# Two changes to a hybrid decoder block: counting in two steps, and the down products at a distance of four FFN tiles

## The chip, the cores and the metric

One core of a Trainium2 chip runs the whole kernel in one launch. The metric is the device time of that launch in microseconds (us). The engines are TensorE (PE; its weight loads are shown as PEld), VectorE (DVE), ScalarE (ACT), GpSimd (POOL) and SyncE (SP), which issues every DMA here. Runs of one kernel lie close together, so the median of three is compared.

## What is computed

One decoder layer for 2048 tokens of width 1024, in float32:

```python
h = rms(x, norm1_g); proj = h @ w_in                      # u, q, k, v, qi, ki, wi, gates
y_ssm = s5_branch(u, ...)                                 # state-space scan, then a GLU
iscore = sum_h relu(qi_h . ki) * wi_h                     # indexer scores, causal
idx = top_k(iscore, 256)                                  # per query, 256 keys
y_att = softmax(q . k[idx]) @ v[idx]                      # 8 heads on the chosen keys
x = x + (sigmoid(g_ssm) * (y_ssm @ w_proj_ssm)
         + sigmoid(g_att) * (y_att @ w_proj_attn)) @ w_out
h2 = rms(x, norm2_g)
x = x + (silu(h2 @ w_ffn_gate) * (h2 @ w_ffn_up)) @ w_ffn_down   # d_ff = 2816
```

## The kernel before

**Products.** Each float32 operand is kept as a rounded part and a remainder, and each product is three TensorE passes (`mm3`, line 406): high by high, high by low, low by high.

**Stages.** `phase1` computes the projections. Then three generators are interleaved by a planner (`Pace`, line 52): the state-space branch, the attention branch, and the dense part. The planner keeps an estimated time for each engine; each generator yields a condition, and the planner lets the first one go on whose condition holds by these estimates. The result is a fixed order of instructions for each engine; the engines follow it and wait on semaphores. A generator that yields `idle("DVE")` goes on when the estimated DVE time is at most `AHEAD` (2.5, later 7 us) ahead of PE's.

**The top-k search.** For a group of four query tiles, `topk` computes the scores `S` of a tile of 128 queries (tile i has (i+1)*128 keys), and finds the 256th largest score of each query by a search over 31 bits. Each bit needs a count of the scores at or above a trial value. Two tiles of a group are "wide": ACT counts them by a Sign activation with an accumulator, and DVE updates the trial value (`un`, then `tr`). The other two are "narrow": DVE counts them, on the high 16 bits of the scores (`H`, as bf16) and then on the low 16 (`H`, as uint16). `count` (line 849) is one `tensor_scalar` over the whole width, with an accumulator; its elementwise output goes to a scratch tile `jkd`. There are four searches: tiles 2 and 3, 4 to 7, 8 to 11, 12 to 15, with narrow widths of 384, of 640 and 768, of 1152 and 1280, and of 1664 and 1792 keys. After a search, `fin` steps (a count of the scores above the threshold, a scan to rank ties, some elementwise steps) make a bias row, and attention of that group follows.

**The dense part.** `block` handles 512 tokens (`tb` 0 to 3): products of the two branches with their projections (`f<-act,ww`), w_out (`f<-ww,mg`), the second norm (its tiles are `ha`, `hb`, `hh`), then 22 FFN tiles f of 128 columns. `up(f, acts)` makes the 48 products of gate and up for one f, and ACT and DVE turn them into an activation tile `at` (DVE step `t`, ACT cast, DVE remainder). `down(acts, last)` multiplies a pair of activation tiles with the two matching rows of w_ffn_down (48 products) and DVE adds each result to `x1`. The loop over c issues up(2c), then down of the pair before, then up(2c+1). Three `at` tiles are kept (pool `fa`).

**Weights.** `weights` lists the loads of a block in one queue, in the order of use; `Rings` hands them out to two rings of buffers: `w` with three tiles, `d` (w_ffn_down, a pair of rows each) with one tile (two in block 3). The queue is first in, first out: a load whose ring is full holds back those behind it. In block 0 a weight is loaded raw, split by POOL, ACT or DVE into its two parts and stored; the later blocks load the stored copies `wc`.

Of the kernel before, what the change touches and what calls it, by code (L numbers as in the profile page):

```python
# [18 lines left out]
ALU = mybir.AluOpType  # L19
# [15 lines left out]
NF = DFF // 128  # L35
# [330 lines left out]
class Block:  # L366
# [431 lines left out]
    def topk(self, st, groups, KL):  # L798

        nc, at, idle = self.nc, self.pace.at, self.pace.idle  # L800
# [35 lines left out]
        S = {}  # L836
        states = []
        for j, (tiles, wide) in enumerate(groups):
# [3 lines left out]
            n = len(tiles)  # L842
# [3 lines left out]
        self.spare_banks = 4  # L846
        jka, jkd = (qp.tile([128, L], BF16, name=n, tag="R") for n in ("jka", "jkd"))

        def count(x, i, t, c):

            nc.vector.tensor_scalar(jkd[:, :(i + 1) * 128], x, t, 0.0, op0=ALU.is_ge, op1=ALU.add, accum_out=c)

        def search(j, tiles, b, wide):

# [83 lines left out]
        for j, (tiles, b) in enumerate(states):  # L938
            n = len(tiles)
            tr = qp.tile([128, n], I32, name="trf")  # L940
            gt = qp.tile([128, n], F32, name="gt")
            fx = qp.tile([128, n], I32, name="fx")
            sg = qp.tile([128, n], I32, name="sg")
            sg2 = qp.tile([128, n], F32, name="sg2")
            ss = qp.tile([128, n], F32, name="ssum")
            nT = qp.tile([128, n], F32, name="nT")
            bf = b.bitcast(F32)
            yield idle("DVE")
            for q, i in enumerate(tiles):
                W = (i + 1) * 128  # L950
                nc.vector.tensor_scalar(jkd[:, :W], S[i], bf[:, q:q + 1], 0.0, op0=ALU.is_gt, op1=ALU.add,
                                        accum_out=gt[:, q:q + 1])
            nc.vector.tensor_scalar(fx, gt, float(TOPK), None, op0=ALU.is_ge)
            nc.vector.tensor_scalar(sg2, b, 0.0, None, op0=ALU.is_ge)
            nc.vector.tensor_scalar(sg, sg2, 2.0, -1.0, op0=ALU.mult, op1=ALU.add)
            nc.vector.tensor_tensor(tr, b, sg, op=ALU.add)
            nc.vector.copy_predicated(b, fx, tr)
            nc.vector.tensor_scalar(nT, bf, -1.0, None, op0=ALU.mult)

            todo = deque(enumerate(tiles))  # L960
            halves = deque()

            def sign():
                nonlocal order
                if todo:
                    q, i = todo.popleft()
                    W = (i + 1) * 128
                    sv, ev = (fin[:, order % 2, z, :W] for z in range(2))
                    order += 1
                    nc.scalar.activation(sv, S[i], AF.Sign, bias=nT[:, q:q + 1], scale=1.0,  # L970
                                         accum_out=ss[:, q:q + 1])
                    halves.append((q, i, W, sv, ev))
            yield idle("ACT", nT)
            sign()
            while halves:
                q, i, W, sv, ev = halves.popleft()
                yield idle("DVE", ss)
                sign()
                nc.vector.tensor_scalar(ev, sv, 0.0, None, op0=ALU.is_equal)
                nc.vector.tensor_tensor_scan(S[i], ones.to_broadcast([128, W]), ev, 0.0, op0=ALU.mult, op1=ALU.add)  # L980
                yield idle("DVE")
                r = qp.tile([128, 1], F32, name="r")
                r2 = qp.tile([128, 1], F32, name="r2")
                nc.vector.tensor_scalar(r2, gt[:, q:q + 1], -1.0, float(TOPK), op0=ALU.mult, op1=ALU.add)
                nc.vector.scalar_tensor_tensor(r, ss[:, q:q + 1], float(W - TOPK), gt[:, q:q + 1],
                                               op0=ALU.add, op1=ALU.subtract)
                nc.vector.tensor_scalar(r, r, -1.0, None, op0=ALU.mult)
                nc.vector.copy_predicated(r2, fx[:, q:q + 1], r)
                nc.vector.scalar_tensor_tensor(ev, S[i], r2, ev, op0=ALU.is_gt, op1=ALU.mult)
                yield idle("DVE")  # L990
                nc.vector.tensor_tensor(ev, ev, sv, op=ALU.subtract)
                nc.vector.tensor_scalar(ev, ev, 0.0, -BIG, op0=ALU.max, op1=ALU.mult)
                yield at("SP", ev)
                nc.sync.dma_start(self.bias_d[i], ev)
# [646 lines left out]
    def weights(self):  # L1641

        a = self.a
        items = []
        for ct in range(KD):
            items.append(("w", lambda raw, ct=ct: [
                (raw[:, i * 512:(i + 1) * 512].rearrange("p (k c) -> p k c", k=4),
                 a[w][0, :, ct * 128:(ct + 1) * 128].rearrange("(k p) c -> p k c", p=128))
                for i, w in enumerate(("w_proj_ssm", "w_proj_attn"))]))
        for cg in range(4):  # L1650
            for b in range(2):
                items.append(("w", lambda raw, cg=cg, b=b: [
                    (raw.rearrange("p (k c) -> p k c", k=4),
                     a["w_out"][0, b * 512:(b + 1) * 512, cg * 256:(cg + 1) * 256]
                     .rearrange("(k p) c -> p k c", p=128))]))
        for f in range(NF):
            for w in ("w_ffn_gate", "w_ffn_up"):
                items.append(("w", lambda raw, f=f, w=w: [
                    (raw.rearrange("p (k c) -> p k c", k=KD),
                     a[w][0, :, f * 128:(f + 1) * 128].rearrange("(k p) c -> p k c", p=128))]))  # L1660

            n = f if f % 2 == 0 else f + 1 if f == NF - 1 else 0
            for q in range(max(n - 2, 0), n):
                items.append(("d", lambda raw, q=q: [(raw, a["w_ffn_down"][0, q * 128:(q + 1) * 128])]))
        copies = [self.dram.tile([128, 2, 1024], F32, name=f"wc{i}") for i in range(len(items))]
        return [(kind, parts, copy, tb > 0) for tb in range(NB) for (kind, parts), copy in zip(items, copies)]
# [8 lines left out]
    def block(self, tb, bigp, ld, nps, nd):  # L1675

        nc, a, at = self.nc, self.a, self.pace.at
        n = TB
# [5 lines left out]
        with ExitStack() as st:  # L1684
# [28 lines left out]
            with ExitStack() as sm:  # L1713
# [123 lines left out]
                yield ready(*hT)  # L1837
                yield from up0(0, (2, 3))
                self.pace.tight = False
            ap = self.pool(st, "fa", 3)  # L1840
            tp = self.pool(st, "ft", 2)
            ld.ring("d", self.pool(st, "fd", nd), nd, 2)

# [63 lines left out]
                if last:  # L1907
                    out(nt - 1)

            prev = None  # L1910
            for c in range(NF // 2):
                acts = []
                for f in (2 * c, 2 * c + 1):
                    acts.append(ap.tile([128, 2, n], F32R, name="at"))
                    yield from up(f, acts[-1])
                    if f % 2 == 0 and prev:
                        yield from down(prev, False)
                prev = acts
            if tb + 1 < NB:
                self.act = [self.load_branch(bigp, br, tb + 1) for br in range(1 + (self.attended >= 4 * (tb + 2)))]  # L1920
            yield from down(prev, True)
            more.close()
            self.lent = False
            del ld.pools["d"]
# [78 lines left out]
```

## Time and profile before

| | |
|---|---|
| median of 3 runs | 3424.11 us (3422.59 to 3427.55) |
| profiled execution | 3425.84 us, of which the span is 3424.1 us |
| busy, share of the span | PE 93%, PEld 78%, DVE 63%, ACT 37%, POOL 19% |
| mean granted TensorE clock | 0.971 of full speed |

```profile
PE   6999989898978999987899999989899999999999
DVE  5565686665886666889777667987766664322222
POOL 3323676521222212343100000001000000000000
PEclk8999999999999999998999999989999999999999
```

Each digit is the busy share of one fortieth of the span (85.6 us) in tenths; PEclk is the granted TensorE clock in tenths of full speed. PE has work nearly all the time, and it dips where DVE is fullest. The searches lie at about 390 to 470 us, 800 to 1000 us, 1405 to 1700 us and 2120 to 2390 us; blocks 0 to 3 start at 984, 1648, 2303 and 2957 us.

### The profile page before, as it was taken

The numbers are of one execution on the slowest core, as the hardware profiler recorded it, in microseconds if no ns is written. First come the engines' busy times: TensorE is split into PE (matmuls) and PEld (weight loads), VectorE is DVE, ScalarE is ACT, GpSimd is POOL, SyncE is SP. The second block draws the span as 40 slices with busy tenths as digits, with TensorE's granted clock in tenths as the row PEclk, the third lists the DMA queues.
The fourth block names the chain that finished last, engine by engine and source line by source line (L and its number), as shares of the span: only waits on it lengthen the run. The fifth ranks groups of instructions, "written<-read, shape, count | busy, mean of one in ns | idle before, by whom it ended". The sixth has DMA issues, their size and how long they took to land. (4 is left out here: it accounts for less than half of the span.)

```text
span 3424.1 us, 43974 instructions
## 1 busy us (share of the span) xinstructions
PE 3179.7 (93%) x16292; PEld 2684.6 (78%) x16292; DVE 2150.5 (63%) x4299; ACT 1262.8 (37%) x2192; POOL 638.6 (19%) x631
## 2 busy tenths in 40 slices
PE   6999989898978999987899999989899999999999
PEld 5889768677757887775788887768788888798887
DVE  5565686665886666889777667987766664322222
ACT  3141545454732444463024444761234342010000
POOL 3323676521222212343100000001000000000000
PEclk8999999999999999998999999989999999999999
DMA  4834433445368656566762334456453333755544
GB/s 134 250 114 117 127 106 108 157 121 156 108 222 289 225 179 226 198 239 249 262 225 112 140 108 171 165 209 227 183 187 131 115 110 141 302 207 200 205 165 183
DMA packets 321527, 605.68 MB, mean 177 GB/s; under 512 B 52896, under 2 KB 205216, under 8 KB 290592
## 3 DMA queue, kind: packets, MB, share of 16 engines
q1 hardware_dynamic: 321312, 602.86, 50.3%
q8 instruction: 129, 2.11, 0.2%
q14 instruction: 86, 0.70, 0.1%
HBM read 434.71 MB, written 166.89 MB: 176 GB/s over the span
## 5 line engine op out<-in xcount | busy, mean ns | idle before, releaser
L206 PE MATMUL f<-h,ww 128*128 128x512 f32 (+1 forms) x4416 | 1011.6, 383 | 3.9 <-DVE x L206 2.2
L206 PEld LDWEIGHTS f<-h,ww 128*128 128x128 f32 x4416 | 800.1, 190 | 160.1 <-POOL ww L206 3.4
L206 PE MATMUL f<-wd,at 128*128 128x512 f32 x2112 | 529.5, 402 | 63.9 <-ACT at L206 34.9
L206 PEld LDWEIGHTS f<-wd,at 128*128 128x128 f32 x2112 | 402.3, 194 | 160.0 <-ACT at L206 27.9
L206 PE MATMUL gps<-hT,gw 128*128 128x512 f32 x1536 | 383.6, 400 | 11.2 <-ACT gsg L206 10.0
L206 ACT ACTIVATE jka<-S,tr 128x1024 bf16<-128x1024 f32 (+6 forms) x217 | 305.8, 1409 | 181.5 <-DVE tr L206 135.8
L206 PEld LDWEIGHTS gps<-hT,gw 128*128 128x128 f32 x1536 | 285.3, 191 | 75.2 <-ACT gsg L206 12.1
L206 DVE TENSOR_TENSOR x<-f,x 128x512 f32<-128x512 f32 x352 | 237.3, 687 | 90.9 <-PE f L206 90.2
L206 DVE SCALAR_TENSOR_TENSOR t<-t,f 128x512 f32<-128x512 f32 (+1 forms) x124 | 82.4, 664 | 329.8 <-PE f L206 285.0
L206 PE MATMUL mm<-w,hT 128*128 128x512 f32 (+1 forms) x1152 | 282.0, 402 | 7.5 <-DVE hT L206 7.3
L206 PEld LDWEIGHTS mm<-w,hT 128*128 128x128 f32 x1152 | 242.1, 241 | 32.9 <-DVE hT L206 9.0
L206 DVE TENSOR_TENSOR tl<-pt,th 128x512 fp32r<-128x512 f32 (+1 forms) x288 | 184.2, 659 | 133.3 <-ACT th L206 132.0
L206 ACT CAST th<-pt 128x512 fp32r<-128x512 f32 (+1 forms) x288 | 155.9, 563 | 233.7 <-PE pt L206 231.7
L206 PE MATMUL f<-act,ww 128*128 128x512 f32 x768 | 189.8, 409 | 29.1 <-DMA act<-act 8.8
L206 POOL TENSOR_TENSOR g<-g,g 128x512 f32<-128x512 f32 x31 | 40.0, 1291 | 916.8 <-issue 553.1
L206 PE MATMUL f<-ww,mg 128*128 128x256 f32 x1536 | 193.5, 288 | 17.5 <-DMA ww<-wc 6.7
L206 PEld LDWEIGHTS f<-ww,mg 128*128 128x128 f32 x1536 | 190.3, 196 | 19.8 <-issue 7.7
L206 PEld LDWEIGHTS f<-act,ww 128*128 128x128 f32 x768 | 150.9, 199 | 67.9 <-issue 10.9
L206 ACT ACTIVATE P<-P,m 128x1024 f32<-128x1024 f32 (+7 forms) x192 | 172.2, 900 | 69.2 <-DVE m L206 68.8
L206 PE MATMUL lg<-kk,q 128*128 128x512 f32 (+1 forms) x640 | 183.9, 389 | 3.4 <-DMA kk<-kk 2.8
L206 ACT ACTIVATE t<-f 128x512 f32<-128x512 f32 (+1 forms) x92 | 53.0, 576 | 332.0 <-PE f L206 331.9
L206 ACT CAST at<-t 128x512 fp32r<-128x512 f32 (+1 forms) x92 | 55.3, 601 | 324.9 <-DVE t L206 324.9
(355 smaller groups left out, 4512.4 us busy)
## 6 DMA issues: line engine op xcount, KB each, us to landing
ww<-wc SPq DMA_DIRECT2D x180, 1024.0 KB, 5.0
wd<-wc SPq DMA_DIRECT2D x66, 1024.0 KB, 8.3
wc<-ww SPq DMA_DIRECT2D x60, 1024.0 KB, 7.8
raw<-in_w_in_dram SPq DMA_DIRECT2D x104, 256.0 KB, 3.4
wc<-wd SPq DMA_DIRECT2D x22, 1024.0 KB, 7.4
x<-in_x_dram SPq DMA_DIRECT2D x32, 512.0 KB, 5.5
gate<-gsg SPq DMA_DIRECT2D x64, 256.0 KB, 2.2
g<-gate SPq DMA_DIRECT2D x64, 256.0 KB, 5.2
```

The costliest lines, as they stand in the source:

```text
L206: return f(*args, **kw)
```

## The change

`count` works in two steps. A `tensor_scalar` without an accumulator compares the first half of the keys and writes 0 or 1 into `jkd`; a `scalar_tensor_tensor` compares the second half, adds that `jkd` elementwise, and accumulates the sum. The count after a search (is greater) goes the same way.

In the dense part two pairs of activation tiles wait in a queue: after up(2c) the product of the pair before the last one is issued, and after the last up both remaining pairs follow, one behind the other. Five `at` tiles are kept. The loads of w_ffn_down stand two f later in the queue, and the last four rows stand together at its end.

```diff
--- before.py
+++ after.py
@@ -846,9 +846,11 @@
         self.spare_banks = 4
         jka, jkd = (qp.tile([128, L], BF16, name=n, tag="R") for n in ("jka", "jkd"))
 
-        def count(x, i, t, c):
-
-            nc.vector.tensor_scalar(jkd[:, :(i + 1) * 128], x, t, 0.0, op0=ALU.is_ge, op1=ALU.add, accum_out=c)
+        def count(x, i, t, c, op=ALU.is_ge):
+
+            h = (i + 1) * 64
+            nc.vector.tensor_scalar(jkd[:, :h], x[:, :h], t, None, op0=op)
+            nc.vector.scalar_tensor_tensor(jkd[:, h:2 * h], x[:, h:], t, jkd[:, :h], op0=op, op1=ALU.add, accum_out=c)
 
         def search(j, tiles, b, wide):
 
@@ -947,9 +949,7 @@
             bf = b.bitcast(F32)
             yield idle("DVE")
             for q, i in enumerate(tiles):
-                W = (i + 1) * 128
-                nc.vector.tensor_scalar(jkd[:, :W], S[i], bf[:, q:q + 1], 0.0, op0=ALU.is_gt, op1=ALU.add,
-                                        accum_out=gt[:, q:q + 1])
+                count(S[i], i, bf[:, q:q + 1], gt[:, q:q + 1], ALU.is_gt)
             nc.vector.tensor_scalar(fx, gt, float(TOPK), None, op0=ALU.is_ge)
             nc.vector.tensor_scalar(sg2, b, 0.0, None, op0=ALU.is_ge)
             nc.vector.tensor_scalar(sg, sg2, 2.0, -1.0, op0=ALU.mult, op1=ALU.add)
@@ -1659,8 +1659,7 @@
                     (raw.rearrange("p (k c) -> p k c", k=KD),
                      a[w][0, :, f * 128:(f + 1) * 128].rearrange("(k p) c -> p k c", p=128))]))
 
-            n = f if f % 2 == 0 else f + 1 if f == NF - 1 else 0
-            for q in range(max(n - 2, 0), n):
+            for q in range(max(f // 2 * 2 - (4 if f % 2 == 0 else 2), 0), f - 2 if f % 2 == 0 else NF if f == NF - 1 else 0):
                 items.append(("d", lambda raw, q=q: [(raw, a["w_ffn_down"][0, q * 128:(q + 1) * 128])]))
         copies = [self.dram.tile([128, 2, 1024], F32, name=f"wc{i}") for i in range(len(items))]
         return [(kind, parts, copy, tb > 0) for tb in range(NB) for (kind, parts), copy in zip(items, copies)]
@@ -1837,7 +1836,7 @@
                 yield ready(*hT)
                 yield from up0(0, (2, 3))
                 self.pace.tight = False
-            ap = self.pool(st, "fa", 3)
+            ap = self.pool(st, "fa", 5)
             tp = self.pool(st, "ft", 2)
             ld.ring("d", self.pool(st, "fd", nd), nd, 2)
 
@@ -1907,18 +1906,19 @@
                 if last:
                     out(nt - 1)
 
-            prev = None
+            pairs = deque()
             for c in range(NF // 2):
                 acts = []
                 for f in (2 * c, 2 * c + 1):
                     acts.append(ap.tile([128, 2, n], F32R, name="at"))
                     yield from up(f, acts[-1])
-                    if f % 2 == 0 and prev:
-                        yield from down(prev, False)
-                prev = acts
+                    if f % 2 == 0 and len(pairs) == 2:
+                        yield from down(pairs.popleft(), False)
+                pairs.append(acts)
             if tb + 1 < NB:
                 self.act = [self.load_branch(bigp, br, tb + 1) for br in range(1 + (self.attended >= 4 * (tb + 2)))]
-            yield from down(prev, True)
+            yield from down(pairs.popleft(), False)
+            yield from down(pairs.popleft(), True)
             more.close()
             self.lent = False
             del ld.pools["d"]
```

The planner makes another order of it. Three places follow; every engine issues the same arithmetic on PE as before.

On PE, in block 0, the first scores of the second attention (`lg<-kk,q`; `f<-ww,mg` are the w_out products, `f<-h` those of gate and up). Before:

```order
L206 MATMUL f<-act_9345,ww 128x512 x12
L206 MATMUL f<-act_9313,ww 128x512 x12
L206 MATMUL f<-act_9345,ww 128x512 x12
L206 MATMUL f<-ww,mg 128x256 x168
L206 MATMUL lg<-kk,q 128x512 x2
L206 MATMUL lg<-kk,q 128x256 x2
L206 MATMUL f<-ww,mg 128x256 x12
L206 MATMUL lg<-kk,q 128x512 x2
```

Now the same place reads:

```order
L206 MATMUL f<-h_9803,ww 128x512 x12
L206 MATMUL f<-h_9802,ww 128x512 x12
L206 MATMUL f<-h_9803,ww 128x512 x12
L206 MATMUL f<-h_9802,ww 128x512 x12
L206 MATMUL lg<-kk,q 128x512 x2
L206 MATMUL lg<-kk,q 128x256 x2
L206 MATMUL f<-h_9803,ww 128x512 x6
L206 MATMUL lg<-kk,q 128x512 x2
```

They stood among the w_out products of block 0 and stand now among its first gate and up products; all that depends on them (the second attention, and the third search behind it) moved back by about as much.

On DVE, in block 2, the second norm (`ha`, `hb`, `hh` are normed rows, `h` their transposed remainders, `x` an update of the residual; `fin` and `S<-ones,fin` belong to the steps behind the fourth search, `jkd` to a count). Before:

```order
L206 SCALAR_TENSOR_TENSOR hb<-x_20251,rr_21027,gB 128x1024
L206 SCALAR_TENSOR_TENSOR x_20251<-f,x_20251 128x2x256
L206 TENSOR_TENSOR h_20591<-f,h_20591 128x4x128
L206 TENSOR_TENSOR h_20592<-f,h_20592 128x4x128
L206 TENSOR_TENSOR h_20591<-f,h_20591 128x4x128
L206 TENSOR_TENSOR h_20592<-f,h_20592 128x4x128
L206 TENSOR_SCALAR ss_21116<-ss_21116 128x1
L206 TENSOR_SCALAR ss_21121<-ss_21121 128x1
L206 SCALAR_TENSOR_TENSOR hh<-x_20251,rr_21117,gB 128x1024
L206 SCALAR_TENSOR_TENSOR hh<-x_20251,rr_21122,gB 128x1024
L206 TENSOR_SCALAR fin<-fin 128x1920
L206 SCALAR_TENSOR_TENSOR S_18668<-ones,fin 128x1920
```

Now the same place reads:

```order
L206 SCALAR_TENSOR_TENSOR hb<-x_20334,rr_21166,gB 128x1024
L206 SCALAR_TENSOR_TENSOR x_20334<-f,x_20334 128x2x256
L206 TENSOR_TENSOR h_20688<-f,h_20688 128x4x128
L206 TENSOR_TENSOR h_20689<-f,h_20689 128x4x128
L206 TENSOR_TENSOR h_20688<-f,h_20688 128x4x128
L206 TENSOR_TENSOR h_20689<-f,h_20689 128x4x128
L206 TENSOR_SCALAR ss_21255<-ss_21255 128x1
L206 TENSOR_SCALAR ss_21260<-ss_21260 128x1
L206 SCALAR_TENSOR_TENSOR hh<-x_20334,rr_21256,gB 128x1024
L206 SCALAR_TENSOR_TENSOR hh<-x_20334,rr_21261,gB 128x1024
L206 TENSOR_SCALAR jkd<-H_19591,tf_19537 128x832
L206 SCALAR_TENSOR_TENSOR jkd,cnt_19536<-H_19591,tf_19537,jkd 128x832
```

The fourth search ended ahead of this norm, and a scan over 1920 keys stood in it; now the search still runs there and a count of two steps stands in its place.

On SP, at the end of block 2, the loads of w_ffn_down (`wd`), of the next block's weights (`ww`) and of the next block's branch activations (`act0`, `act1`); `out` stores the result, `g` loads gates. Before:

```order
L206 DMA wd_25472<-wc77_9305 128x2x1024
L206 DMA ww_25502<-wc78_9306 128x2048
L206 DMA ww_25533<-wc79_9307 128x2048
L206 DMA wd_25628<-wc80_9308 128x2x1024
L206 DMA wd_25628<-wc81_9309 128x2x1024
L206 DMA ww_25631<-wc0_9228 128x2048
L206 DMA ww_25660<-wc1_9229 128x2048
L206 DMA ww_25689<-wc2_9230 128x2048
L206 DMA act0_25694<-act3_185 128x2x512 x4
L206 DMA act1_25699<-att3_189 128x2x512 x4
L206 DMA out_0_dram<-x1_20251 128x1024 x4
L206 DMA g0_25791<-gate0_1_135 128x512
```

Now the same place reads:

```order
L206 DMA wd_25689<-wc79_9321 128x2x1024
L206 DMA act0_25837<-act3_185 128x2x512 x4
L206 DMA att3_189<-yh_25899 128x4x128
L206 DMA att3_189<-ya_24715 128x4x128
L206 DMA wd_25935<-wc80_9322 128x2x1024
L206 DMA wd_25935<-wc81_9323 128x2x1024
L206 DMA ww_25938<-wc0_9242 128x2048
L206 DMA ww_25940<-wc1_9243 128x2048
L206 DMA ww_25942<-wc2_9244 128x2048
L206 DMA out_0_dram<-x1_20334 128x1024 x4
L206 DMA g0_26032<-gate0_1_135 128x512
L206 DMA act1_26034<-att3_189 128x2x512 x4
```

The last pair of `wd` loads stood ahead of the last up and stands now behind `act0`, right before the next block's first weights; `act1` stood ahead of the stores and stands now behind them.

## Rows read from the trace of the kernel before

**Rows 1.** Page, busy time: busy us (share of the span), instructions.

```profile
PE 3179.7 (93%) x16292; PEld 2684.6 (78%) x16292; DVE 2150.5 (63%) x4299; ACT 1262.8 (37%) x2192; POOL 638.6 (19%) x631
```

**Rows 2.** Stretches: length, then busy PE, PEld, DVE, ACT, POOL, clock, DMA share, GB/s.

```profile
380.00:520.00 140.00, 125.68 (x615) 97.49 (x614) 114.36 (x311) 73.07 (x164) 97.46 (x157) 1.00 0.33 97
1406.00:1648.00 242.00, 197.96 (x798) 156.99 (x797) 217.14 (x388) 114.60 (x149) 96.35 (x46) 0.91 0.66 230
1648.00:1791.00 143.00, 131.84 (x801) 118.37 (x802) 96.45 (x166) 23.09 (x39) 13.49 (x12) 0.96 0.66 241
2120.00:2303.00 183.00, 160.30 (x676) 129.32 (x675) 170.64 (x350) 130.84 (x137) 0.30 (x1) 0.95 0.50 189
2303.00:2459.00 156.00, 136.72 (x801) 122.25 (x802) 115.34 (x173) 30.75 (x45) 13.50 (x12) 0.92 0.59 215
2957.00:3092.00 135.00, 129.60 (x803) 116.30 (x802) 35.84 (x55) 17.07 (x31) 13.43 (x12) 0.99 0.69 258
```

**Rows 3.** Timeline of PE in block 3: start, us, engine, operation, [idle before, releaser].

```profile
3091.74 11.04 PE L206 MATMUL f<-wd,at 128*128 128x512 f32 x48
...
3124.38 11.04 PE L206 MATMUL f<-wd,at 128*128 128x512 f32 x48
```

**Rows 4.** Timeline of PE in block 1, during the fourth search.

```profile
2120.30 21.95 PE L206 MATMUL f<-h,ww 128*128 128x512 f32 x96
...
2286.20 12.60 PE L206 MATMUL f<-wd,at 128*128 128x512 f32 x45 [9.06 <-ACT at L206]
```

**Rows 5.** Timeline of PE, last down products of block 0 and of block 2.

```profile
1633.75 13.20 PE L206 MATMUL f<-wd,at 128*128 128x512 f32 x45 [15.54 <-ACT at L206]
...
2946.30 10.74 PE L206 MATMUL f<-wd,at 128*128 128x512 f32 x45 [0.82 <-ACT at L206]
```

**Rows 6.** DVE by form, 2120 to 2303 us: count | busy us, mean ns.

```profile
L206 DVE TENSOR_SCALAR_CACHE_REDUCE jkd<-H,tr 128x1792 bf16<-128x1792 bf16 x15 | 31.1, 2076 | 0.2
...
L206 DVE SCALAR_TENSOR_TENSOR tr<-un,tr 128x1 int32<-128x1 int32 x59 | 9.4, 160 | 2.0
```

**Rows 7.** DVE by form, 1406 to 1648 us.

```profile
L206 DVE SCALAR_TENSOR_TENSOR tr<-un,tr 128x1 int32<-128x1 int32 x62 | 38.8, 626 | 2.1
L206 DVE TENSOR_SCALAR_CACHE_REDUCE jkd<-H,tr 128x1280 bf16<-128x1280 bf16 x15 | 23.1, 1539 | 0.1
```

**Rows 8.** Timeline of DVE, two `fin` steps over 2048 keys.

```profile
2390.15 0.69 DVE L206 TENSOR_SCALAR fin<-fin 128x2048 bf16<-128x2048 bf16 x1 [0.97 <-ACT fin L206]
...
2395.90 2.35 DVE L206 SCALAR_TENSOR_TENSOR fin<-S,r,fin 128x2048 bf16<-128x2048 f32 x1
```

**Rows 9.** DVE by form, 380 to 520 us: the same two steps, narrower.

```profile
L206 DVE SCALAR_TENSOR_TENSOR fin<-S,r,fin 128x384 bf16<-128x384 f32 x1 | 0.6, 618 | 0.0
...
L206 DVE TENSOR_SCALAR fin<-fin 128x512 bf16<-128x512 bf16 x2 | 0.7, 336 | 2.7 <-ACT fin L206 2.7
```

**Rows 10.** Timeline of DVE and POOL from 1449 us, in the third search.

```profile
1449.65 1.89 POOL L206 TENSOR_TENSOR ww<-raw,zeros 128x1024 fp32r<-128x1024 f32 x1 [8.49 <-PE f L206]
1449.77 1.54 DVE L206 TENSOR_SCALAR_CACHE_REDUCE jkd<-H,tr 128x1280 bf16<-128x1280 bf16 x1
...
1451.62 2.41 POOL L206 TENSOR_TENSOR ww<-raw,ww 128x1024 fp32r<-128x1024 f32 x1
...
1451.87 2.18 DVE L206 SCALAR_TENSOR_TENSOR tr<-un,tr 128x1 int32<-128x1 int32 x1
```

**Rows 11.** Timeline of SP at the end of block 2.

```profile
2933.95 1.18 SPq L206 DMA_DIRECT2D wd<-wc  x2
```

**Rows 12.** DMA issues from 2930 to 2990 us: KB each, median us to landing.

```profile
wd<-wc SPq DMA_DIRECT2D x2, 1024.0 KB, 6.2
...
act<-att SPq DMA_DIRECT2D x4, 512.0 KB, 10.4
```

**Rows 13.** Timeline of DVE and PE in the norm of block 2.

```profile
2420.25 4.16 DVE L206 TENSOR_TENSOR_SCAN S<-ones,fin 128x1920 f32<-128x1920 f32 x1
...
2425.05 1.97 PE L206 MATMUL f<-ident,hh 128*128 128x128 f32 x8 [5.91 <-DVE h L206]
```

## Prediction

> **What bounds the kernel now.** I read the page's busy times first: PE is busy 93% of the span [rows 1], so the change can only pay where PE waits or runs at a lower granted clock. Then a table of stretches [rows 2]: the two late searches stand out, 198 us of PE work in 242 us and 160 in 183, at a mean granted clock of 0.91 and 0.95 (mostly the level of 2.4 GHz, in part 1.2), with DVE busy for 217 and 171 of them. Undisturbed, PE needs 32.64 us for a pass of two ups and a down, 144 products (from 3091.74 to 3124.38) [rows 3], or 0.2267 us a product. By that the 798 products of the third search's stretch are worth 181 us, so 61 are lost there; the 676 of the fourth's are worth 153, so 30 are lost. Block starts without a search take 135 us, with one 143 and 156 [rows 2]: 8 and 21 lost.
>
> Next, which wait ends last. At the ends of blocks 0 and 1 PE waits 15.54 and 9.06 us for the activation tile of the last f [rows 4, 5], whose DVE step stands behind counts. In the passes ahead of it PE waits for banks that DVE has not emptied: from 2120.30 to 2286.20 less the 9.06 are 156.8 us, and the 627 products in it (four passes, 48 and 3) are worth 142.1; 14.7 are lost.
>
> **The counts.** A one-pass count takes 2.08 us at 1792 keys and 1.54 at 1280 [rows 6, 7], about 1.05 ns a key, so 1.94 at 1664, 1.40 at 1152, 0.60 at 384. No row shows the two new steps; the nearest are the `fin` steps. A tensor_scalar of bf16 took 0.34 us at 512 and 0.69 at 2048, a scalar_tensor_tensor 0.62 at 384 and 2.35 at 2048 [rows 8, 9]. On lines through these, half of 1792 keys costs 0.42 + 1.15 = 1.57, a saving of 0.50; 1664 saves 0.45, 1280 0.29, 1152 0.23, and 384 costs 0.26 + 0.42 = 0.68, 0.08 more. Half of the counts read uint16, and for a dense uint16 tensor_scalar there is no row. Its bounds are the bf16 line (0.42) and the scalar_tensor_tensor's (1.15), with which the count would be 0.2 slower; I take 0.42, since it reads as many bytes. The Trainium skill, "VectorE: DVE Perf Modes", "What auto-detection actually checks", goes by 16-bit type and step and not by bf16, which would give the same; no run here shows it. Over 31 bits and two tiles DVE gets back 29 us in the fourth search, 16 in the third, some 4 in the second, and loses 2.5 in the first.
>
> **What speaks against it.** POOL works for 97 of 140 us in the first search and 96 of 242 in the third, and for 0.3 of 183 in the fourth [rows 2]. A `tr` step, a scalar_tensor_tensor of one element a partition, takes 160 ns in the fourth search and 626 in the third [rows 6, 7]. One began 0.25 us into a POOL subtraction and ended with it, after 2.18 us. The one-pass count that began 0.12 us into another POOL step took its usual 1.54 [rows 10]. So two-input DVE steps are held while POOL works, and the one-pass count is not. The second new step has two inputs and is exposed; I take the first to be exposed too, since it is of the fast form. The Trainium skill states the rule ("SBUF — State Buffer", "SBUF: two separate sides"): a DVE operation that uses both ports, or reads two SBUF inputs, and a GpSimd operation exclude each other for their whole length; the traces agree with it for `tr` (626 against 160 ns). By the rule both steps are held, which is the slower rival below; were it not so, the hold terms here would be zero.
>
> The hold is 0.47 us for one exposed step at the third search's POOL share; a count has two, the second usually just behind the end of the hold, so 0.47 to 0.94 for the pair. I take 0.47, the row as it is. In the first search a count then loses 0.08 and some 0.5 by the same row: over 33 counts 20 us on DVE. Other PE work is interleaved there, DVE is busy 114 of 140 us, and I let 8 of the 20 reach PE (0 to 20).
>
> **What moves.** The second attention begins among the first gate and up products instead of the w_out products, some 65 us of PE work later, and the third search with it. By the order 50 of its 66 counts stood ahead of the end of block 0 and 16 in the start of block 1; now 30 and 36. Of the fourth search's counts 44 of 66 stood in block 1, now 29, and 37 fall into the start of block 2.
>
> - Third search in block 0: 61 us lost now, 45 without the 15.54. For 30 counts of 50 that is 27, plus hold 30 x 0.47 = 14 less the saving 30 x 0.26 = 8: 33. At the end the last two downs stand together. The first needs an older activation tile, and its 10.9 us cover the late DVE step. The second needs `wd`, whose one buffer is free only when the first has ended, and which is split anew there: POOL took 1.89 and 2.41 us for the two parts of such a tile [rows 10], the pair has two tiles, so 4.3 us shared out and 8.6 in a row; I take 6. 39 instead of 61: **-22** (-45 to +5).
> - Start of block 1: 8 lost with 16 counts, now 36 and the activation steps of the wide tiles: 14. **+6** (-5 to +20).
> - Fourth search in block 1: 30 lost now, 21 without the 9.06. For 29 counts of 44 it is 14; DVE, busy 171 of 183, gets 14 us free there, and I take half of the 14, 7. At the end `wd` is loaded: the two loads landed 6.2 us after their issue (median, rows 12) when they went out 12 us ahead of the product that waits [rows 5, 11]; now they go out when their buffer falls free, behind the first down, with the activation loads in flight, and PE waits 8 (6 to 10.4, the slowest median there). 15 instead of 30: **-15** (-25 to 0).
> - Start of block 2: 21 lost, of which 5.91 behind one scan of 4.16 us in the norm [rows 13]. The scans are gone from it, counts of 1.5 us stand there: **-6** (-20 to +10).
> - The `fin` steps of the third and fourth search now lie between ups and downs, with scans of 4 us ahead of evictions: **+4** (0 to 10).
> - End of block 2: 0.82 us of wait and a little more now [rows 5], then the `wd` loads as above: **+6** (4 to 10).
> - Start of block 3: `act1` was issued ahead of the last down; now it stands behind the stores on SP, since the last attention ends later. It landed 10.4 us after issue [rows 12]; the two products ahead of its first use cover 24 x 0.2267 = 5.4, SP's issues add 2: **+7** (0 to 10).
> - Start of block 0: 19 counts of the second search and its `fin` steps move into it. No row prices that: **+4** (-5 to +15).
> - Last block: both activation tiles are long ready at the end: **-1**.
>
> In all 8 - 22 + 6 - 15 - 6 + 4 + 6 + 7 + 4 - 1 = -9 us. Against the profiled execution's 3425.84 us that is 3416.8; it lay 1.7 above the median, so the forecast is **3415 us**. PE's arithmetic is the same, so everything else stays.
>
> **The rivals.**
> (a) POOL's hold decides (slower). Place: the first three searches. Each of the two steps is held, and POOL's weight splits are held in turn, so weights come late for PE. Price: the first search's whole 20 instead of 8, 7 in the second, 28 instead of 14 in the third, and 8 for late weights: 41 more, 3456. It decides once a two-step count in the third search takes over 1.9 us on average in block 0. For it: 626 against 160 ns. Against it: other PE work fills the first search.
> (b) The search's savings don't reach PE (near no change, or a little slower): the wide tiles on ACT set its length, the planner fills DVE as before, and the loss per pass stays. Then the fourth search gives 8 instead of 15, the third 14 instead of 22, block 2's start nothing: 3436 at worst, 3428 if one of the three holds. For it: ACT is busy 131 of 183 us. Were the uint16 step slow, the outcome is this one too: the change then does not make counts shorter.
> (c) The waits for activations were the root of more: with them gone DVE's backlog stops hurting, third search -35, fourth -22, block 2's start -12: 3389.
>
> **How the numbers follow.** About 0.2%, 7 us, is what a measurement of this kernel can tell from no change. The forecast has 0.50, its own range 3395 to 3428 (faster 0.36, same 0.12, slower 0.02). (a) has 0.20, slower. (b) has 0.20, of which 0.09 is same and 0.11 slower. (c) has 0.10, faster. Faster 0.46, same 0.21, slower 0.33. The range 3383 to 3449 takes in (b), nearly all of (c) and the lower half of (a).
>
> **What would show it.** In the profile after: `jkd` tensor_scalar of 0.4 and scalar_tensor_tensor of 1.1 us at 832 and 896 keys, and longer means where POOL works; no wait for `at` ahead of the last downs, but one for `wd` of 6 to 10 us at the ends of blocks 1 and 2 and a shorter one in block 0; a wait for `act1` at the start of block 3; passes in the fourth search of under 35 us. It is wrong if the passes stay at 36, if the first search's stretch grows by more than 15 us, or if block 0 ends later than 1650 us.

## The result, and the profile after

The changed kernel takes 3391.95 us (median of 4 runs, 3387.57 to 3394.26) against 3425.83 us of the kernel before in the same set: a ratio of 0.9898, 95% interval 0.988 to 0.9915. It is 34 us faster. 9 us faster was forecast: the time lies in the whole range (3383 to 3449), and some 3 us below the forecast's own part of it (3395 to 3428). Its page, busy times, for [rows 1]:

```profile
PE 3179.1 (94%) x16292; PEld 2687.4 (79%) x16292; DVE 2118.4 (62%) x4540; ACT 1277.2 (38%) x2210; POOL 622.4 (18%) x620
```

PE does the same work in 33 us less span. Where they went is read from the starts of the four blocks on PE, in both traces; each part holds the same number of products in both:

| part | before, us | after, us | difference | forecast |
|---|---|---|---|---|
| up to block 0 | 984.5 | 989.6 | +5.1 | +8 |
| block 0 | 663.3 | 642.4 | -20.9 | -18 |
| block 1 | 655.5 | 636.4 | -19.1 | -7 |
| block 2 | 653.6 | 656.0 | +2.4 | +2 |
| block 3 to the end | 467.2 | 466.4 | -0.8 | +6 |

(The forecast's +4 for the `fin` steps is shared between blocks 1 and 2.) The stretches that answer to [rows 2], after: length, busy PE, PEld, DVE, ACT, POOL, clock, DMA share, GB/s. They are the first search, the third from its first counts to the end of block 0, the start of block 1, and the fourth search from its first counts to the end of block 1.

```profile
380.00:520.00 140.00, 127.12 (x587) 98.64 (x586) 118.51 (x336) 70.16 (x155) 97.70 (x153) 0.94 0.32 94
...
1470.00:1632.00 162.00, 133.30 (x534) 105.18 (x532) 149.30 (x306) 90.12 (x116) 69.62 (x30) 0.92 0.68 240
1632.00:1798.00 166.00, 154.31 (x896) 137.19 (x897) 119.55 (x282) 46.24 (x69) 13.48 (x12) 0.96 0.60 223
2160.00:2268.00 108.00, 100.17 (x429) 81.61 (x428) 88.38 (x241) 82.74 (x87) 0.84 (x1) 0.97 0.60 225
```

At 0.2267 us a product, 162 - 534 x 0.2267 = 41 us are lost in the third search in block 0 (61 before, 39 forecast), and 108 - 429 x 0.2267 = 11 in the fourth in block 1 (30 before, 15 forecast). The new steps in that fourth search, DVE by form (count | busy us, mean ns):

```profile
L206 DVE SCALAR_TENSOR_TENSOR jkd<-H,tr,jkd 128x896 bf16<-128x896 bf16 x12 | 13.8, 1151 | 0.4
L206 DVE SCALAR_TENSOR_TENSOR tr<-un,tr 128x1 int32<-128x1 int32 x38 | 6.1, 160 | 1.3
...
L206 DVE TENSOR_SCALAR jkd<-H,tr 128x896 bf16<-128x896 bf16 x12 | 5.4, 449 | 0.1
```

The first step on uint16, DVE by form, 2268 to 2434 us:

```profile
L206 DVE TENSOR_SCALAR jkd<-H,tf 128x896 bf16<-128x896 uint16 x16 | 7.2, 452 | 0.5
```

A count of 1792 keys takes 0.45 + 1.15 = 1.60 us (forecast 1.57) for 2.08 [rows 6]. uint16 takes the short time too, as the Trainium skill has it in "VectorE: DVE Perf Modes", "What auto-detection actually checks": 452 ns beside 449.

The ends of the blocks, for [rows 4, 5], timeline of PE:

```profile
1609.18 0.51 PE L206 MATMUL f<-wd,at 128*128 128x512 f32 x1 [2.03 <-POOL wd L206]
1611.68 1.22 PE L206 MATMUL f<-wd,at 128*128 128x512 f32 x2 [2.00 <-POOL wd L206]
1614.05 0.80 PE L206 MATMUL f<-wd,at 128*128 128x512 f32 x1 [1.15 <-POOL wd L206]
1618.27 11.92 PE L206 MATMUL f<-wd,at 128*128 128x512 f32 x44 [3.43 <-DVE un L206]
...
2253.91 1.62 PE L206 MATMUL f<-wd,at 128*128 128x512 f32 x3 [5.47 <-DVE un L206]
2256.46 12.15 PE L206 MATMUL f<-wd,at 128*128 128x512 f32 x45 [0.94 <-DMA wd<-wc]
...
2908.60 1.62 PE L206 MATMUL f<-wd,at 128*128 128x512 f32 x3 [5.36 <-DMA wd<-wc]
2911.15 12.47 PE L206 MATMUL f<-wd,at 128*128 128x512 f32 x45 [0.93 <-DMA wd<-wc]
...
2933.87 0.97 PE L206 MATMUL f<-act,ww 128*128 128x512 f32 x3 [1.92 <-DMA act<-att]
```

Beside the wait at 1618.27, timeline of DVE:

```profile
1617.01 1.21 DVE L206 TENSOR_TENSOR wd<-raw,wd 128x1024 fp32r<-128x1024 f32 x1
```

No last product waits for its activation tile any more. It waits for `wd` instead. In blocks 1 and 2 that is 6.4 and 6.3 us, for the two loads in turn (`un`, named at 2253.91, is no input of these products; the loads, issued from 2248.5 on, landed 5.3 and 7.3 us later). In block 0 it is 8.6 us in four pieces: three behind POOL's parts of the split, and 3.43 for the second tile's remainder, which stands behind counts on DVE and ends at 1618.22 (`un` is again no input). At the start of block 3 the `act<-att` waits are 1.9 us and less.

So far all of the forecast's signs but one, the shorter `wd` wait in block 0, could be read as confirmed. The experiments show that the cause was another one.

### The profile page after: what moved, and what is told of

Its sections match the earlier page's. It is cut to its first block, busy times and chain, and to the rows that moved or that the text cites. A ratio compares the mean times of both kernels' runs of the same rounds, so it can differ in the third digit from the quotient of the medians.

```text
span 3390.8 us, 44218 instructions
## 1 busy us (share of the span) xinstructions
PE 3179.1 (94%) x16292; PEld 2687.4 (79%) x16292; DVE 2118.4 (62%) x4540; ACT 1277.2 (38%) x2210; POOL 622.4 (18%) x620
## 5 line engine op out<-in xcount | busy, mean ns | idle before, releaser
L206 PE MATMUL f<-wd,at 128*128 128x512 f32 x2112 | 521.1, 399 | 42.8 <-DVE un L206 16.0
L206 ACT ACTIVATE jka<-S,tr 128x1536 bf16<-128x1536 f32 (+5 forms) x217 | 305.6, 1408 | 193.6 <-DVE tr L206 119.2
```

The lines of the kernel that those rows point to most:

```text
L206: return f(*args, **kw)
```

## The experiments

**The theories.** *Counts*: shorter counts give DVE time back in the late searches. *Distance*: the activation waits were the root. *Order*: the gain is the new order of instructions, since the planner prices a count by its form, and the two forms have other prices. These lines of the planner (87 to 95) set the price; on DVE r is 1.05 ns a column, and `short` holds where the operands are of 16 bits:

```python
cost = size * r + c
...
if eng == "DVE" and op in ("tensor_copy", "tensor_scalar", "memset") and "accum_out" not in kw:
    if all(z.space != PSUM for z in aps):
        cost -= size * r * (0.75 if short else 0.5)
elif eng == "DVE" and op in ("tensor_scalar", "tensor_tensor") and short:
    cost -= size * r / 2
if "accum_out" in kw:
    cost += 0.2 if eng == "ACT" else 0.14
```

The one-pass count of 1792 16-bit keys is priced at half a column, 1.15 us; the trace has 2.08 [rows 6]. The two steps are priced at a quarter of a column and at a whole one, for half of the keys each: 0.31 + 1.15 us and a gap of 0.15 between them, 1.61; the trace has 1.60. "Price" below is that of 1792 keys.

**All runs.** Each ratio is to the kernel before in the same set; parts in us of the profiled execution. The parts hold the same products in every run but e11, where 16 move from block 1 to block 2.

| run | price, us | counts | distance | ratio (95%) | up to block 0 | block 0 | 1 | 2 | 3 to end |
|---|---|---|---|---|---|---|---|---|---|
| before | 1.15 | one pass | 2 | 1 | 984 | 663 | 656 | 654 | 467 |
| after | 1.61 | two steps | 4 | 0.9898 (0.988-0.9915) | 990 | 642 | 636 | 656 | 466 |
| e1 | 1.61 | two steps | 2 | 0.9902 (0.988-0.9923) | 989 | 663 | 631 | 646 | 468 |
| e2 | 1.15 | one pass | 4 | 1.0046 (1.003-1.0062) | 982 | 681 | 654 | 667 | 460 |
| e3 | 1.15 | two steps | 2 | 0.9972 (0.9961-0.9984) | 997 | 674 | 639 | 645 | 464 |
| e4 | 1.61 | one pass | 2 | 0.9897 (0.9877-0.9917) | 981 | 645 | 647 | 654 | 467 |
| e5 | 1.61 | one pass | 4 | 0.9882 (0.9866-0.9899) | 982 | 628 | 643 | 667 | 466 |
| e6 | 1.61 | two steps late | 2 | 0.9857 (0.9842-0.9871) | 978 | 644 | 639 | 648 | 466 |
| e7 | 2.09 | one pass | 2 | 0.9842 (0.9827-0.9856) | 975 | 631 | 637 | 656 | 469 |
| e8 | 0.68 | one pass | 2 | 1.0239 (1.022-1.0259) | 1005 | 691 | 696 | 645 | 466 |
| e9 | 1.61, others true | two steps late | 2 | 0.9799 (0.9784-0.9815) | 978 | 631 | 634 | 647 | 466 |
| e10 | 1.61, others true | two steps late | 4 | 0.9823 (0.9805-0.9841) | 974 | 641 | 636 | 653 | 460 |
| e11 | 3.03 | one pass | 2 | 1.0073 (1.0054-1.0091) | 962 | 629 | 631 | 757 | 471 |
| e12 | 2.11 | one pass | 2 | 0.988 (0.9865-0.9896) | 970 | 640 | 636 | 666 | 469 |

**e1, e2: one part of the change alone.** The count's lines of the diff alone, and the lines of the distance alone.

> Counts in two steps, the products of w_ffn_down as before (a distance of two FFN tiles, three activation tiles). Theory of the counts (VectorE's shorter counts give back most of what the third and fourth searches lose): about 3407 us, 15 to 20 below 3426, with the fourth search (block 1) losing about 12 us of PE time instead of 30, and the 15.5 us wait of the last products of block 0 still there. Rival of the distance (all from activation tiles that came late): 3424 to 3430, no gain. Rival of the order (the planner merely drew a better order): any time, but the same as that of the one-pass counts in this same order (run e4).

> Distance of four FFN tiles and five activation tiles, counts in one pass. Theory of the counts: about 3415 us, 8 to 12 below 3426 (the 15.5 us and 9.1 us waits ahead of the last products of blocks 0 and 1 go, waits of about 5 us for w_ffn_down's rows come at the ends of two blocks), with the fourth search still losing 25 to 30 us of PE time. Rival of the distance: 3390 to 3396, all of the gain. Rival of the order: a time that follows no wait named here.

e1: 3396.77 us, nearly the whole gain and 10 more than the theory of the counts gave it. e2: 3444.21 us, slower, where that theory had 3415 and the theory of the distance 3390 to 3396. The theory of the distance falls. e2's third search, from its first counts to the end of block 0, in the columns of the stretches above:

```profile
1395.00:1663.00 268.00, 213.54 (x847) 169.58 (x847) 242.65 (x426) 116.73 (x152) 102.17 (x48) 0.90 0.62 218
```

Its trace has 60 narrow counts in this stretch, 7.1 to 100 products, where before had 50 on 798, 6.3. 268 - 847 x 0.2267 = 76 us are lost, for 61. The activation wait at the end of block 0 is gone, but PE then waits about as long for a bank, since the DVE step that empties it stands behind counts. e2's timeline of PE:

```profile
1660.19 2.93 PE L206 MATMUL f<-wd,at 128*128 128x512 f32 x6 [13.26 <-DVE x L206]
```

I read both waits as DVE's backlog: the distance changed only where PE meets it.

**e3, e4: counts and order apart.** e3 issues two steps and notes one pass in the planner, so that every other instruction stands where it stood before. e4 notes two steps and issues one pass: the order is e1's. The traces bear that out: PE, ACT and POOL run the same instructions in the same order in e3 and before, in e4 and e1, and in the pairs of one order below. The main lines of e4:

```diff
-            nc.vector.tensor_scalar(jkd[:, :(i + 1) * 128], x, t, 0.0, op0=ALU.is_ge, op1=ALU.add, accum_out=c)
+            h, note = (i + 1) * 64, self.pace.note
+            note("DVE", "tensor_scalar", (jkd[:, :h], x[:, :h], t, None), dict(op0=op))
+            note("DVE", "scalar_tensor_tensor", (jkd[:, h:2 * h], x[:, h:], t, jkd[:, :h]), dict(op0=op, accum_out=c))
+            nc.vector.eng.tensor_scalar(jkd[:, :2 * h], x, t, 0.0, op0=op, op1=ALU.add, accum_out=c)
```

> Counts in two steps as in e1, but priced in the planner as the one pass was, so that the order of the instructions on every engine is that of the kernel before (each one-pass count replaced by its two steps in place); distance as before. This is what the shorter counts are worth by themselves. Theory of the counts: 3405 to 3415 us. Rival of the order: 3424 to 3430, no gain, since only the reshuffled order helped. If the hold by GpSimd decided, above 3430.

> Counts in one pass, but priced in the planner as the two steps, so that the order of the instructions is that of e1; distance as before. This is what the order alone is worth. Theory of the counts: 3424 to 3432 us, no gain. Rival of the order: near 3407, as e1.

e4 takes 3395.26 us: the old counts at the old distance, in the new order, have the whole gain. e3 takes 3420.01, 7 less than before, between what the two theories gave it (3405 to 3415, and 3424 to 3430): with the same order, 29.5 us are had in blocks 1 to 3 and 23 are lost ahead of them. The fourth search, from its first counts to the end of block 1, in e4, e3 and e1, in that order:

```profile
2140.00:2272.00 132.00, 122.43 (x531) 99.82 (x530) 118.14 (x256) 100.16 (x106) 0.29 (x1) 0.97 0.56 212
```

```profile
2143.00:2310.00 167.00, 156.32 (x673) 127.56 (x672) 149.42 (x400) 129.62 (x137) 0.84 (x1) 0.97 0.55 208
```

```profile
2158.00:2283.00 125.00, 121.06 (x530) 98.62 (x528) 104.24 (x290) 99.59 (x106) 0.84 (x1) 1.00 0.57 212
```

Lost are 12, 14 and 5 us; before, 30 [rows 2]. Either remedy, a thinner order or shorter counts, takes away about half of the loss or more: e4 has 30 one-pass counts on 531 products (5.6 to 100), e3 has 46 shorter ones on 673 (6.8, as before). At the old distance the order alone also shortens the activation waits, from 15.54 and 9.06 us to 6.63 and 6.32. e4's timeline of PE, end of block 0:

```profile
1613.03 12.31 PE L206 MATMUL f<-wd,at 128*128 128x512 f32 x45 [6.63 <-ACT at L206]
```

Of the 30 lost before, 7 were products that ran longer (160.30 us busy for 153), at a granted clock of 0.95; in e1 it is 1, at 1.00.

**e5, e6: the hold.** e5 issues e4's one pass in the changed kernel's order. e6 is e1 with the two steps only `if i >= 12` (tiles 12 to 15, the fourth search), and the same order.

> The changed kernel with its counts in one pass, priced in the planner as the two steps: the order of every engine is the changed kernel's. What the two steps are worth in the changed kernel. The earlier pair (same order, two steps against one: +8.6 us before block 0, +18.7 in block 0, -16.2 in block 1, -8.0 in block 2) gives 3386 to 3392 us here: about 980 at the start of block 0, 624 in block 0, 650 and 664 in blocks 1 and 2. Theory that the counts made the gain: 3410 to 3425.

> The order and distance of the count-alone run; the two steps only for tiles 12 to 15 (the fourth search, while GpSimd is idle), one pass for tiles 0 to 11 (while GpSimd works beside the counts). Theory of the hold (VectorE's two-input steps are held while GpSimd works, the one-pass counts are not): 3365 to 3375 us, the start of block 0 at 981, block 0 at 645 (as the one-pass run in this order), blocks 1 and 2 at 631 and 646 (as the two-step run). Rival (the two runs of this order differ by something else than the hold): 3390 to 3397, as both of them.

e5 takes 3386.5 us, no slower than the changed kernel: all in all the changed kernel's two steps give nothing, they cost 22 us ahead of block 1 and give 18 in blocks 1 and 2. e6 takes 3376.89, 2 us above its range, where e1 and e4 in the same order take 3397 and 3395. Its parts up to block 0's end are e4's and block 2 is near e1's; block 1, at 639 us, lies between e1's 631 and e4's 647. The reason shows when e1 and e4 are laid side by side, product by product. e1 is 7.6 us behind after the first search, 16 at 1050 us (the last counts of the second search stand there, beside POOL, with single steps of up to 2.6 us), 27 at the end of block 0, 18 after the third search and 3 after the fourth. So the steps that cost time beside POOL already pay in block 1, where 29 of the third search's counts run and POOL is busy for only 10 of 89 us, and e6 gives these up. The third search's counts in e1, then in e4 (ns: min/median/max):

```profile
L206 DVE TENSOR_SCALAR jkd<-H,tr x30: 355/376/2078, 1492.8 to 1619.4; 128x576 bf16<-128x576 bf16 x15, 128x640 bf16<-128x640 bf16 x15
L206 DVE SCALAR_TENSOR_TENSOR jkd<-H,tr,jkd x30: 817/883/2935, 1494.5 to 1621.1; 128x576 bf16<-128x576 bf16 x15, 128x640 bf16<-128x640 bf16 x15
```

```profile
L854 DVE TENSOR_SCALAR_CACHE_REDUCE jkd<-H,tr x30: 1399/1470/1548, 1471.7 to 1593.6; 128x1152 bf16<-128x1152 bf16 x15, 128x1280 bf16<-128x1280 bf16 x15
```

Each kind of new step is held by up to 2 us; no one-pass count is. Timeline of DVE and POOL in the changed kernel:

```profile
1502.95 1.89 POOL L206 TENSOR_TENSOR ww<-raw,zeros 128x1024 fp32r<-128x1024 f32 x1 [14.06 <-PE f L206]
1503.12 1.89 DVE L206 TENSOR_SCALAR jkd<-H,tr 128x576 bf16<-128x576 bf16 x1
1504.92 2.40 POOL L206 TENSOR_TENSOR ww<-raw,ww 128x1024 fp32r<-128x1024 f32 x1
1505.04 2.89 DVE L206 SCALAR_TENSOR_TENSOR jkd<-H,tr,jkd 128x576 bf16<-128x576 bf16 x1
```

The first step, 0.36 us by itself, and the second, 0.82, both end after the POOL step beside them. That is the rule of the Trainium skill ("SBUF — State Buffer", "SBUF: two separate sides") for the fast form (the first step) and for two inputs (the second), and the trace agrees for both.

**e7, e8, e11, e12: the price by itself.** The kernel before, with nothing but the planner's price of a count changed: a column at 1.05, 0.26 and 1.575 ns, and the true price with 0.02 us more.

```diff
-            nc.vector.tensor_scalar(jkd[:, :(i + 1) * 128], x, t, 0.0, op0=ALU.is_ge, op1=ALU.add, accum_out=c)
+            W = (i + 1) * 128
+            self.pace.price = [1.05e-3 * W + 0.21]
+            nc.vector.tensor_scalar(jkd[:, :W], x, t, 0.0, op0=op, op1=ALU.add, accum_out=c)
```

(The lines that hand this price to the planner are left out.)

> The kernel before, its one-pass counts unchanged, but priced in the planner at what the trace shows (1.05 ns a column and 0.21 us: 2.09 us at 1792 columns, where the trace has 2.076) and not at half a column. Theory of the price (counts priced at half their time are packed too densely beside TensorE's work): 3385 to 3400 us, as the order with a price of 1.6 us gave, or better. Rival (each reshuffle draws a time at random): anywhere from 3380 to 3440, with no relation to the price.

> The kernel before, its one-pass counts unchanged, priced in the planner at 0.26 ns a column and 0.21 us (0.68 us at 1792 columns, a third of the trace's 2.076). Theory of the price: slower than before, 3435 to 3470 us, block 0 above 663 us. Rival of the random draw: anywhere from 3380 to 3440, as likely faster as slower.

> The kernel before, one-pass counts, priced in the planner at 1.575 ns a column and 0.21 us, half above what the trace shows (3.03 us at 1792 columns for 2.08). Theory of the true price: the gain has been had, 3365 to 3395 us, no better than the true price's 3372 beyond what an order draws (and the late tail grows, since fewer counts fit ahead of the products of block 2). Rival (more spread is always better): 3345 to 3362.

> The true price with 0.23 us for its constant in place of 0.21: no count's price changes by more than 3 per cent, but ties in the planner fall otherwise and the order of every engine is reshuffled. What an order drawn anew is worth by itself. Theory of the price: within 10 us of 3372. Rival of the random draw: as far from it as the kernels of the other prices were, 20 to 50 us.

They take 3372.26, 3508.22, 3452.28 and 3384.75 us. e7 is 13 us better than the range named for it ("or better" was left open), and e8 is 38 worse; both lie on the side that the theory of the price names. The third and fourth search in e8, then in e7:

```profile
1416.00:1696.00 280.00, 220.33 (x864) 173.33 (x863) 251.52 (x468) 121.65 (x158) 95.14 (x46) 0.88 0.60 213
2120.00:2392.00 272.00, 219.46 (x881) 174.28 (x879) 245.44 (x463) 144.05 (x153) 0.29 (x1) 0.91 0.42 158
```

```profile
1402.00:1606.00 204.00, 184.64 (x774) 147.52 (x773) 181.23 (x333) 114.62 (x150) 93.86 (x43) 0.97 0.75 262
2136.00:2243.00 107.00, 102.61 (x444) 83.76 (x443) 91.54 (x201) 81.34 (x86) 0.29 (x1) 0.98 0.54 204
```

e8 loses 84 and 72 us, with 7.2 and 7.0 narrow counts to 100 products; e7 28 and 6, with 4.1 and 4.7. Too high a price costs as well, elsewhere: e11 starts block 2 21 us ahead of e7 (16 products, worth some 4 us, moved behind that point), but so many counts are put off that the fourth search ends when block 2 has hardly a product left, and PE does the last attention alone, from here to 2979 us (timeline of PE):

```profile
2689.80 10.04 PE L206 MATMUL f<-wd,at 128*128 128x512 f32 x43
2716.05 1.19 PE L206 MATMUL lg<-kk,q 128*128 128x512 f32 x2 [16.20 <-DMA kk<-kk]
```

Here I expected 3365 to 3395; that the tail would grow was expected, but not by 100 us. So the true price is the best of those tried, and e11 adds that a thinner spread of counts helps only as long as products are left to cover them. e12 misses its 10 us by 2.5: an order drawn anew at nearly the same price was worth 12.5 us, in this one draw. Differences of that size between two orders prove nothing; the fall from 3508 over 3425 and 3395 to 3372, taken as a whole, does.

**e9, e10: both remedies, at either distance.** e7's price for tiles 0 to 11, two steps at their own price for 12 to 15; e10 adds the distance.

> Distance of two FFN tiles. Counts of tiles 0 to 11 in one pass at the true price of the run before (1.05 ns a column and 0.21 us), counts of tiles 12 to 15 in two steps at the planner's own price for them. Theory of price and hold together: start of block 0 and block 0 as with the true price alone (975 and 631), blocks 1 and 2 shorter by what two steps gave there in one order (8 to 16 and 6 to 9 us, less now that the counts are spread): 3352 to 3366 us. Rival (with counts at a true price VectorE is no longer what ends last, so shorter counts give nothing): 3368 to 3376.

> The run before it (true price, two steps for tiles 12 to 15) with the distance of four FFN tiles and five activation tiles. What the distance is worth once the price is true. Theory (the distance removes an end-of-block wait of some 6 us in block 0 and brings waits for w_ffn_down's rows of about 5 us at the ends of blocks 1 and 2): within 8 us of the run before it. Rival (the distance alone cost 16 us in the old order because of itself): 12 us or more slower than the run before it.

e9 takes 3357.41 us, the best of all, some 15 below e7 by the ratios. Their orders differ, so this alone does not show that shorter counts still pay where POOL is idle; e6 against e4 shows it, some 14 us by the ratios in one order. e9 beats the changed kernel too, by more than an order drawn anew (0.9799, 0.9784 to 0.9815, against 0.9898). e10 takes 3365.82, 8.4 above e9, just past the 8 of its theory. Over the four pairs that differ by the distance and the order that follows from it, the ratios make it worth +16 (before, e2), -1 (e1, after), -5 (e4, e5) and +8 us (e9, e10). No steady worth of the distance itself is shown. Its one steady mark is the `wd` wait; in e10 at the end of block 2:

```profile
2888.62 1.62 PE L206 MATMUL f<-wd,at 128*128 128x512 f32 x3 [6.10 <-DMA wd<-wc]
```

## Why the forecast was right, and where it was wrong

The direction was right, and the range held the time, but in part by luck: only the range's lower end, put there for rival (c), reaches down to 3392, and (c)'s mechanism is not what the runs show.

By cause the forecast's -9 is made of three sums. *The move of counts*: -18 in the third search (27 lost for 45), +6, -7 in the fourth (14 for 21), -6, +4 for `fin`, +4 at block 0: -17. *The steps themselves*: +8 in the first search, +6 in the third (hold less saving), -7 in the fourth: +7. *The distance*: -9.5, -1 in the fourth search, +6, +7 and -1: about +1.

- **The step that failed is the move** ("What moves" and the losses scaled from it). The order alone is worth -32 us (e4), not -17; with the distance, in the changed kernel's own order, it is -39 (e5) for -16. The term that failed most is the fourth search. It was sized in proportion, 29 counts of 44 and so 14 us of 21 left (by the traces 25 and 46 narrow 16-bit counts); on the same 429 products e5 loses 13 us, of which 6 are the `wd` wait, so 7 are left with the counts unchanged. The start of block 0 (+4) failed too: in e5 all of block 0 is 36 us shorter, and the third search explains only 28 of them. The loss is no price per count: it fell from 4.4 us to 100 products at 6.8 counts to 2.2 at 5.6 and 1.4 at 4.7 (before, e4, e7), and at 6.8 shorter counts it is 2.1 (e3). That fits DVE falling behind the plan. The order was read, but not why it changed: the price 1.15 could have been set beside the row of 2.08 before any run.
- **The fourth search in block 1**, -15: measured 30 to 11, -19; the `wd` wait 6.4 for 8, the rest 4.3 for 7. The size is near, its parts are not: the order gives 17 (30 to 13, e5) and the steps 2, not 7. **The start of block 1**, +6: PE is idle for 11.7 us of the stretch, and was for 11.2 [rows 2], about +1. These two make up 9 of the 12 us by which block 1 came out lower.
- **Third search in block 0**: 41 lost for 39 forecast, the -22 right in size, and in its parts too: on the same products e5 loses 33 us, of which 5.7 are the `wd` wait, so 27 are left, as the proportion had it. The hold was right: 1.80 and 1.62 us measured for 1152 and 1280 keys in the changed kernel, 1.18 and 1.27 without a hold, 0.49 on average for 0.47.
- **The steps themselves**, +7: in the changed kernel's order (e5, then after) they make +7.3 up to block 0, +14.7 in block 0, -7.0 and -11.5 in blocks 1 and 2, about +3.5; in e1's order (e4, then e1) +8.6, +18.7, -16.2 and -8.0, about +3. The sum is near, its terms are not: the hold of the second search's counts in block 0 stands in rival (a) alone, and the saving on the counts of block 2 nowhere.
- **Block 2**: +2.4 for +2 is luck. The order and the distance make +14 (e5), the steps take 11.5 of it back; neither was forecast.
- **First search**: +8 forecast, +5.1 measured for all up to block 0; its counts are held by some 0.28 us and not 0.5.
- **`wd` at the ends**: 6.4 and 6.3 us for 8 and 6 in blocks 1 and 2, right; 8.6 for 6 in block 0, since the last part of the split stands behind counts on DVE. **`act1` in block 3**: +7 forecast, waits of 3.5 us in all, and the part shows -0.8: too dear.
- **The rivals.** The time came near (c), 3389, but not by its mechanism: with the distance alone (e2) the activation waits went and the kernel got slower. (a)'s mechanism is real (e6), but the order outweighs it. (b) falls: e3 gives 29.5 us behind block 0 by the steps alone.

## What to carry to other kernels

Where a planner sets the order, compare its price of each repeated operation with the trace first: correcting one price was worth 53 us here, give or take the dozen that any new order can draw, and more than the rewritten operation. To part an edit from the order that it causes, run the old operation in the new order and the new one in the old. In this kernel the two-step count paid where GpSimd was idle, and the one-pass count with its accumulator was the better one beside GpSimd's work.

## What was not expected of the hardware

A 16-bit one-pass compare with accumulator takes about 1.05 ns a column and 0.2 us (1.54 us at 1280, 2.08 at 1792), while the same compare without accumulator takes 0.45 at 896. The hold goes both ways: POOL's `ww<-raw,zeros` steps in block 0 take 2.19 us on average in e1 and 2.01 in e6, where only the counts differ.
